# Three transformer blocks on one core: two unused tiles shift the moving operands in SBUF

## The chip, the cores and the metric

The kernel runs on one core of a Trainium2 chip. The metric is the device time in microseconds of one launch. The program is one straight sequence per engine: TensorE (PE, with its weight loads as PEld), VectorE (DVE), ScalarE (ACT), GpSimd (POOL) and SyncE (SP, which only issues DMAs). [...]

## The reference

Three blocks work in turn on x, 256 tokens of width 1024, in float32. Cut to what matters:

```
def swiglu(h, w_gate, w_up, w_down):            # d_ff = 2816
    return (silu(h @ w_gate) * (h @ w_up)) @ w_down

# blocks 0 and 1 (i = 0, 1)
x = x + 0.5 * swiglu(rms_norm(x, g[0]), ...)
h = rms_norm(x, g[1])
m = even_mixer(h, ...) if i == 0 else mla_mixer(h, ...)
x = x + m
x = x + 0.5 * swiglu(rms_norm(x, g[2]), ...)
x = x + rms_norm(sigmoid(rms_norm(x, g[3]) @ ple_w_gate) * (p_i @ ple_w_proj), g[4])

# block 2
mixed = concat(block attention, state-space mixer, pooling mixer) of rms_norm(x) @ w_in
x = x + mixed @ w_out
x = x + swiglu(rms_norm(x), ...)
out = rms_norm(x)
```

`even_mixer` has a gated spatial part and a chunked recurrence, `mla_mixer` is an attention with low-rank projections of queries and keys. Most of the arithmetic is the five feed-forward networks (FFNs): 1024 x 5632 for gate and up, 2816 x 1024 for down.

## The kernel before

The activations are kept transposed: x is eight tiles of 128 rows (features) by 256 columns (tokens). The weights, 220 pieces of 128 x 2048 floats in the order of their use, are streamed by SP into three buffers `wraw`. Each half piece is split in two by line 256 (ACT: the rounded part `whi`) and line 257 (DVE: the remainder `wlo`), into six buffers each of 128 x 1024.

Every product of the large projections is three matmuls of type fp32r: high part times high part, low activation times high weight, high activation times low weight. With `mm(out, l, r)` (line 163), l is the stationary operand, loaded by a LDWEIGHTS, and r the moving one. In the rows a matmul stands as `acc<-hh,whi`: the moving tile first, then the stationary tile. Three kinds of projection use it:
- `fm` (gate, up, down and most of the others): stationary is a 128 x 128 slice of `whi` or `wlo`, moving is a 128 x 256 slice of activations, so the result is again transposed. For gate and up the moving tiles are `hh0` to `hh7` (high parts of the normalized rows) and `hl0` to `hl7` (low parts). For down they are slices of `big` tiles, of which each holds the parts of two chunks of the gated product. An FFN has 44 chunks x 8 x 3 = 1056 matmuls in gate and up, and 8 x 22 x 3 = 528 in down.
- `out_proj` (the mixers' output projections): the same, with slices of `big` or, after attention, of `o2` as moving tile (the profile shows it as `o`).
- `tm` (projections whose result stands by tokens): stationary is a 128 x 128 slice of the activations, moving up to 512 columns of `whi` or `wlo`.

The order is as the loops write it, but for a few pieces that `high_priority` and `issue_after` move. In an FFN, gate and up run with two pauses early in the stretch: the sum of squares of x over the features is made on PE with a column of ones (`Stat.begin`), and the resulting scale is spread over the partitions by transposes of `ny` against `ident` (`Stat.finish`, line 299). After that, gate and up, and down behind them, go on without other work on PE; DVE and ACT evaluate what leaves PSUM and split the weights ahead.

Tiles get their place in SBUF by pool, `wp` first, then `cp`, then `sp`, and in a pool in the order in which a name is first asked for; a place is rounded up to 32 bytes per partition. In the built program the bytes per partition are:

```
tiles                                   start modulo 256, before    after
wraw, whi, wlo (wp)                                  128             128
cols (672 bytes, cp)                                 128             128
ones (4 bytes, cp)                                    32              32
x, ident, hh0..hh7, hl0..hl7 (cp)                     64             192
constants behind them, e.g. k_tri                    160              32
gu (sp, first)                                         0             128
sq, sqa, rb, sg, pr, big, o2, as (sp)                  0              64
ae, at (sp)                                          128             192
```

The slices that the matmuls take are multiples of 512 bytes into these tiles (but for a few behind a piece of 390 columns), so the table gives the operands' own places. `constants` (line 168) is where the tiles of the change are asked for; `run` and `build` follow it.

Of the kernel before, what the change touches and what calls it, by code (L numbers as in the profile page):

```python
# [10 lines left out]
FT = mybir.dt.float32  # L11
# [6 lines left out]
P = 128  # L18
# [88 lines left out]
class Kern:  # L107
# [61 lines left out]
    def constants(self):  # L169
        nc, a, cp = self.nc, self.a, self.cp  # L170
        self.cols = cp.tile([P, a["cols"].shape[1]], FT, name="cols")
        self.x = []
        self.raw = [self.wp.tile([P, PIECE], FT, name="wraw", bufs=3) for _ in range(2)]

        def load_x(c, n, eng=nc.sync):
            t = cp.tile([P, n * T], FT, name=f"x{c}")
            eng.dma_start(t, a["xT"][:, c * T : (c + n) * T])
            self.x += [t[:, u * T : (u + 1) * T] for u in range(n)]

        def load_w(i, q, n):  # L180
            o = slice(q * 512, (q + n) * 512)
            nc.sync.dma_start(self.raw[i][:, o], a["wts"][i][:, o])


        self.ones = cp.tile([P, 1], FT, name="ones")
        nc.vector.memset(self.ones, 1.0)
        idle = self.tmp(512, "gu", bufs=3)
        nc.vector.memset(idle, 0.0)
        ps = self.aux()
        for _ in range(5):  # L190
            self.mm(ps[:, :T], idle[:, :P], idle[:, :T])
        load_x(0, 1)
        nc.scalar.dma_start(self.cols, a["cols"])
        load_w(0, 0, 1)
        load_x(1, 1, nc.scalar)
        load_w(0, 1, 1)
        load_x(2, 1, nc.scalar)
        load_w(0, 2, 1)
        load_x(3, 1)
        load_w(0, 3, 1)  # L200
        load_x(4, 2)
        load_w(1, 0, 2)
        load_x(6, 2)
        load_w(1, 2, 2)
        self.ident = cp.tile([P, P], FT, name="ident")
        nc.sync.dma_start(self.ident, a["ident"])
        self.hT = [
            (cp.tile([P, T], FR, name=f"hh{c}"), cp.tile([P, T], FR, name=f"hl{c}"))
            for c in range(D)
        ]  # L210
        self.eps = cp.tile([P, 1], FT, name="eps")
        nc.vector.memset(self.eps, EPS)
        nc.scalar.activation(self.tiny(1, "nz"), self.ones, AF.Silu)
# [1435 lines left out]
```

## Time and profile before

| | before |
|---|---|
| runs | 1342.49, 1348.98, 1348.85 us |
| median | 1348.85 us |
| profiled execution | 1348.33 us |
| its span (first to last instruction) | 1346.5 us |
| PE busy | 1319.8 us, 98% of the span |
| weight loads (PEld) | 1290.1 us, 96% |
| DVE, ACT | 920.6 and 727.1 us |
| matmuls | 10830 |

A matmul's duration in the trace reaches from its start to the modelled end of its result. Successive matmuls overlap, so busy time and mean duration do not tell how fast they follow each other. The number of them in a window does. A float32 matmul that is not fp32r stands as two instructions.

### The profile page before, as it was taken

To read this page: it belongs to the slowest core of one execution; us is meant where nothing else is said; L and a number is where in the kernel's file an instruction comes from. 1 tells how busy PE (TensorE), PEld (TensorE's weight loads), DVE (VectorE), ACT (ScalarE), POOL (GpSimd) and SP (SyncE) were. 2 spreads that over 40 slices of the span, in tenths; PEclk is the share of its full clock that TensorE was granted. 3 is DMA by queue.
4 is the path that set the end of the run, shared out by engine and by line. 5 is a ranking of instruction groups with operands and counts; after the bars stand their busy time and mean duration, and the time that the engine had idled before them with its cause. 6 is when DMAs were issued, how large, how long until landed. Compare 5 with 4: busy or idle time off the path is not lost.

```text
span 1346.5 us, 25894 instructions
## 1 busy us (share of the span) xinstructions
PE 1319.8 (98%) x10830; PEld 1290.1 (96%) x10830; DVE 920.6 (68%) x1528; ACT 727.1 (54%) x1110; POOL 76.7 (6%) x94
## 2 busy tenths in 40 slices
PE   8999999999999999999999899999998999999997
PEld 8999999899999999999999679999998998999997
DVE  6866567968667557866656767766558897866643
ACT  6655446546544456655445666544445675644442
POOL 4000010002000001000010002000002000200001
PEclk9999999999999999999999999999999999999998
DMA  8755455345555453655455324555545343555541
GB/s 313 261 192 205 175 191 186 103 159 182 188 187 198 171 205 126 220 188 188 160 187 193 118 72 148 189 188 188 183 163 188 126 167 119 185 188 188 188 159 61
DMA packets 34933, 235.50 MB, mean 175 GB/s; under 512 B 4016, under 2 KB 4784, under 8 KB 7168
## 3 DMA queue, kind: packets, MB, share of 16 engines
q1 hardware_dynamic: 32976, 229.98, 49.1%
q0 software_dynamic: 832, 2.47, 0.6%
q8 instruction: 85, 1.39, 0.4%
q10 hardware_dynamic: 1008, 1.40, 0.3%
q14 instruction: 32, 0.26, 0.1%
HBM read 232.78 MB, written 1.05 MB: 174 GB/s over the span
## 4 chain that ended last, share of the span: by engine, by line
PE 74%; DVE 5%; ACT 2%; issue 1%; DVEq 0%; ACTq 0%
PE acc L163 70%; PE aux L163 4%; DVE wlo L257 2%; PE aux L299 0%; DVE big L1172 0%; PE aux L1127 0%; ACT whi L256 0%; DVE qs L958 0%; DVE kv L958 0%; DVE big L511 0%; ACT ae L1119 0%; ACT big L946 0%; ACT at L1129 0%; DVE big L1494 0%; DVE nz L293 0%
## 5 line engine op out<-in xcount | busy, mean ns | idle before, releaser
L257 DVE TENSOR_TENSOR wlo<-wraw,whi 128x1024 fp32r<-128x1024 f32 (+1 forms) x440 | 530.3, 1219 | 270.1 <-ACT whi L256 177.0
L256 ACT ACTIVATE whi<-wraw 128x1024 fp32r<-128x1024 f32 (+1 forms) x440 | 451.7, 1048 | 319.3 <-PE acc L163 224.9
L163 PE MATMUL acc<-hh,whi 128*128 128x256 f32 x2192 | 330.7, 281 | 4.1 <-ACT hh L535 3.1
L163 PE MATMUL acc<-hl,whi 128*128 128x256 f32 x2192 | 329.6, 280 | 0.2 <-DVE hl L540 0.2
L163 PE MATMUL acc<-hh,wlo 128*128 128x256 f32 x2192 | 328.8, 280 | 0.2 <-DVE wlo L257 0.2
L163 PEld LDWEIGHTS acc<-hh,whi 128*128 128x128 f32 x2192 | 288.5, 189 | 5.8 <-ACT hh L535 3.8
L163 PEld LDWEIGHTS acc<-hh,wlo 128*128 128x128 f32 x2192 | 288.7, 189 | 0.8 <-DVE wlo L257 0.6
L163 PEld LDWEIGHTS acc<-hl,whi 128*128 128x128 f32 x2192 | 288.6, 189 | 0.4 <-DVE hl L540 0.4
L163 PE MATMUL acc<-big,whi 128*128 128x256 f32 x2032 | 277.9, 283 | 0.0
L163 PEld LDWEIGHTS acc<-big,whi 128*128 128x128 f32 x2032 | 261.6, 189 | 0.4 <-ACT big L267 0.2
L163 PE MATMUL acc<-big,wlo 128*128 128x256 f32 x1016 | 164.8, 283 | 0.0
L163 PEld LDWEIGHTS acc<-big,wlo 128*128 128x128 f32 x1016 | 139.8, 189 | 0.0
L315 POOL TENSOR_TENSOR sqa<-sqa,sq 128x256 f32<-128x256 f32 x72 | 65.5, 910 | 1135.8 <-ACT sq L314 1133.7
L426 DVE TENSOR_TENSOR gu<-acc,rb 128x512 f32<-128x512 f32 (+1 forms) x122 | 81.9, 678 | 51.9 <-PE acc L163 51.9
L270 ACT ACTIVATE hh<-x,cols 128x256 fp32r<-128x256 f32 x64 | 30.3, 503 | 84.2 <-DVE x L465 80.6
L267 ACT ACTIVATE big<-pr 128x256 fp32r<-128x256 f32 x114 | 45.9, 409 | 51.9 <-DVE pr L444 50.1
L442 ACT ACTIVATE sg<-gu 128x256 f32<-128x256 f32 x110 | 44.8, 411 | 38.7 <-DVE gu L426 38.5
L268 DVE TENSOR_TENSOR big<-pr,big 128x256 fp32r<-128x256 f32 x114 | 47.9, 426 | 20.3 <-ACT big L267 20.2
L444 DVE TENSOR_TENSOR pr<-sg,gu 128x256 f32<-128x256 f32 x110 | 45.4, 418 | 2.8 <-ACT sg L442 2.8
L271 DVE SCALAR_TENSOR_TENSOR hl<-x,cols,hh 128x256 fp32r<-128x256 f32 x64 | 36.9, 602 | 8.5 <-ACT hh L270 8.3
L163 PE MATMUL aux<-big 128*128 128x128 f32 (+5 forms) x260 | 37.6, 310 | 1.9 <-DVE big L680 1.7
L314 ACT ACTIVATE sq<-x 128x256 f32<-128x256 f32 x62 | 24.0, 405 | 24.9 <-DVE x L467 18.4
(297 smaller groups left out, 788.1 us busy)
## 6 DMA issues: line engine op xcount, KB each, us to landing
wraw<-wts SPq DMA_DIRECT2D x216, 1024.0 KB, 4.9
wraw<-wts SPq DMA_DIRECT2D x4, 256.0 KB, 5.0
wraw<-wts SPq DMA_DIRECT2D x2, 512.0 KB, 6.5
x<-xT SPq DMA_DIRECT2D x2, 256.0 KB, 5.7
big<-wsT POOLq DMA_DIRECT2D x1, 512.0 KB, 10.4
gu<-pT ACTq DMA_DIRECT2D x2, 256.0 KB, 3.1
out<-big SPq DMA_DIRECT2D x2, 256.0 KB, 2.2
out<-big ACTq DMA_DIRECT2D x2, 256.0 KB, 2.4
```

The lines of the kernel that those rows point to most:

```text
L163: return self.nc.tensor.matmul(out, l, r, start=start, stop=stop, skip_group_check=True).ins
L256: nc.scalar.activation(hi[:, i], s, AF.Copy)
L257: nc.vector.tensor_tensor(lo[:, i], s, hi[:, i].bitcast(FT), op=OP.subtract)
L267: a = nc.scalar.activation(hi, src, AF.Copy)
L268: b = nc.vector.tensor_tensor(lo, src, hi.bitcast(FT), op=OP.subtract)
L270: a = nc.scalar.activation(hi, src, AF.Copy, scale=scale)
L271: b = nc.vector.scalar_tensor_tensor(lo, src, scale, hi.bitcast(FT), op0=OP.mult, op1=OP.subtract)
L314: nc.scalar.activation(q, src, AF.Square)
L315: self.mark = nc.gpsimd.tensor_tensor(self.sq[0], self.sq[0], q, op=OP.add).ins
L426: self.nc.vector.tensor_tensor(out.rearrange("p (u t) -> p u t", u=n), ps.rearrange("p (u t) -> p u t", u=n), rb.unsqueeze(1).to_broadcast ...
L442: self.mark = nc.scalar.activation(sg, gu[:, :T], AF.Silu).ins
L444: nc.vector.tensor_tensor(pr, sg, gu[:, T:], op=OP.mult)
```

## The change

Two tiles are asked for and never used: one of 32 floats (128 bytes per partition) in `cp` behind `ones`, and one of 48 floats (192 bytes) in `sp` behind `gu`. Everything that is asked for later in these pools moves up: the tiles in `cp` behind the first by 128 bytes, `gu` too, and the tiles in `sp` behind the second by 320. The weights stay. All engines have the same instructions in the same order; only the addresses differ, as the table above shows.

```
         self.ones = cp.tile([P, 1], FT, name="ones")
+        cp.tile([P, 32], FT, name="pad")
         nc.vector.memset(self.ones, 1.0)
         idle = self.tmp(512, "gu", bufs=3)
...
             (cp.tile([P, T], FR, name=f"hh{c}"), cp.tile([P, T], FR, name=f"hl{c}"))
             for c in range(D)
         ]
+
+        self.sp.tile([P, 48], FT, name="pad", bufs=1)
         self.eps = cp.tile([P, 1], FT, name="eps")
```

## Rows read from the trace of the kernel before

**Rows 1.** The page's first part: busy us of each engine.
```profile
PE 1319.8 (98%) x10830; PEld 1290.1 (96%) x10830; DVE 920.6 (68%) x1528; ACT 727.1 (54%) x1110; POOL 76.7 (6%) x94
```

**Rows 2.** The chain of waits, two long pieces: start us, us, what.
```profile
321.89 181.99 PE acc L163 x1536
...
550.14 174.82 PE acc L163 x1476
```

**Rows 3.** The page's second part, 40 slices: clock in tenths, GB/s.
```profile
PEclk9999999999999999999999999999999999999998
...
GB/s 313 261 192 205 175 191 186 103 159 182 188 187 198 171 205 126 220 188 188 160 187 193 118 72 148 189 188 188 183 163 188 126 167 119 185 188 188 188 159 61
```

**Rows 4.** The page's groups: line engine op tiles xcount | busy, mean ns | idle.
```profile
L257 DVE TENSOR_TENSOR wlo<-wraw,whi 128x1024 fp32r<-128x1024 f32 (+1 forms) x440 | 530.3, 1219 | 270.1 <-ACT whi L256 177.0
...
L163 PE MATMUL acc<-hh,whi 128*128 128x256 f32 x2192 | 330.7, 281 | 4.1 <-ACT hh L535 3.1
...
L163 PE MATMUL acc<-big,whi 128*128 128x256 f32 x2032 | 277.9, 283 | 0.0
...
L163 PE MATMUL acc<-big,wlo 128*128 128x256 f32 x1016 | 164.8, 283 | 0.0
```

**Rows 5.** Windows: gate/up, down of each FFN: window, length, busy (count), PEclk, ...
```profile
30.00:128.00 98.00, 98.00 (x867) 98.00 (x867) 71.96 (x99) 55.44 (x81) 1.10 (x1) 1.00 0.65 221
131.00:191.00 60.00, 60.00 (x508) 60.00 (x507) 32.27 (x43) 29.82 (x41) 4.42 (x6) 1.00 0.51 179
330.00:428.00 98.00, 98.00 (x835) 98.00 (x834) 64.91 (x88) 49.01 (x69) 0.58 (x1) 1.00 0.56 188
430.00:496.00 66.00, 66.00 (x553) 66.00 (x552) 39.03 (x53) 31.24 (x44) 5.16 (x7) 1.00 0.51 178
560.00:655.00 95.00, 95.00 (x809) 95.00 (x808) 64.76 (x87) 47.73 (x68) 0.00 (x0) 1.00 0.57 193
657.00:717.00 60.00, 60.00 (x502) 60.00 (x502) 30.97 (x36) 27.60 (x38) 4.43 (x6) 1.00 0.50 176
850.00:946.00 96.00, 96.00 (x817) 96.00 (x817) 64.62 (x86) 46.52 (x68) 0.00 (x0) 1.00 0.55 189
949.00:1009.00 60.00, 60.00 (x503) 60.00 (x501) 30.82 (x37) 27.81 (x38) 4.49 (x6) 1.00 0.50 176
1170.00:1271.00 101.00, 101.00 (x860) 101.00 (x859) 68.86 (x90) 49.30 (x72) 0.00 (x0) 1.00 0.54 183
1274.00:1333.00 59.00, 59.00 (x494) 59.00 (x493) 25.18 (x29) 26.58 (x35) 5.51 (x6) 1.00 0.36 126
```

**Rows 6.** Windows, PE alone: two hh stretches (first, third), two output projections.
```profile
215.50:236.90 21.40, 21.40 (x191) 1.00 0.57 197
292.80:303.70 10.90, 10.90 (x94) 1.00 0.45 153
...
531.50:543.00 11.50, 11.50 (x104) 1.00 0.01 3
...
1134.00:1147.90 13.90, 13.90 (x120) 1.00 0.44 152
```

**Rows 7.** The timeline behind a down projection, one by one: start us, us, ...
```profile
498.50 0.28 PE L163 MATMUL acc<-hh,wlo 128*128 128x256 f32 x1
...
501.22 0.28 PE L163 MATMUL acc<-hh,wlo 128*128 128x256 f32 x1
```

**Rows 8.** Matmuls with o2: durations ns min/median/max, first and last start us.
```profile
L163 PE MATMUL acc<-o,whi x176: 274/282/386, 785.2 to 1139.2; 128*128 128x256 f32 x176
...
L163 PE MATMUL acc<-o,wlo x88: 278/283/386, 786.8 to 1139.3; 128*128 128x256 f32 x88
```

**Rows 9.** The timeline where the weights move: start us, us, what xcount.
```profile
1107.24 1.07 PE L163 MATMUL acc<-whi,hl 128*128 128x256 f32 x8
1108.15 1.07 PE L163 MATMUL acc<-wlo,hh 128*128 128x256 f32 x8
...
1113.59 1.10 PE L163 MATMUL acc<-wlo,hh 128*128 128x256 f32 x8
```

More of the change, by code (lines that the diff above doesn't have):

```diff
@@ L185, in constants @@
         self.ones = cp.tile([P, 1], FT, name="ones")
+        cp.tile([P, 32], FT, name="pad")
         nc.vector.memset(self.ones, 1.0)
@@ L210, in constants @@
         ]
+        self.sp.tile([P, 48], FT, name="pad", bufs=1)
         self.eps = cp.tile([P, 1], FT, name="eps")
```

## Prediction

> **What bounds the kernel now.** I read the page's busy shares first: PE 1319.8 us of a span of 1346.5, DVE 920.6, ACT 727.1 [rows 1]. The chain of waits says the same: its longest pieces are nothing but matmuls of line 163, 182 us in a row without a step on another engine [rows 2]. [...] So neither clock nor DMA nor the splitting of the weights (530 us of DVE in all, 1219 ns for each half piece [rows 4]) sets the pace; what counts is the time from one matmul's start to the next.
>
> That step is not on the page, because the durations (281 ns and more) overlap. It comes out of windows cut inside steady stretches. The count x takes in matmuls that merely reach into the window; at a duration of about 280 ns and a step of about 118 ns those are 2.4. So the step is the window's length over (x - 2.4) [rows 5]:
> - gate and up projections (moving: hh or hl): 98/864.6 = 113.35 ns in the first FFN, then 117.7, 117.8, 117.8, 117.8 ns in the other four;
> - down projections (moving: big): 60/505.6 = 118.7 ns in the first, then 119.9, 120.1, 119.9, 120.0 ns.
>
> All of these are 128x256 with a 128x128 weight load beside each. [...] The output projections, with big or o2 as moving tile, take 10.9/91.6 = 119.0 and 13.9/117.6 = 118.2 ns. Shorter hh stretches outside the FFNs, 21.4/188.6 = 113.5 and 11.5/101.6 = 113.2 ns [rows 6]. An error of one in the count is 0.5 to 1% in these.
>
> Set beside the addresses: the weights stand at 128 modulo 256, hh and hl at 64 (192 ahead of the weights, or 64 behind), big and o2 at 0 (128 from them). Distance 64 has two levels, 113.4 and 117.8; distance 128 has two others, 118.7 and 120.0. The four FFNs at 117.8 run the same loops at the same addresses as the one at 113.4, so a level is not given by address alone. In the rows it holds to the end of a stretch, and it passes into the down projection: the only 113.4 is followed by the only 118.7. The opposite step is not a copy: the hh stretch that begins straight after a down projection of 120 ns runs from 498.50 to 501.22, 24 steps (the alternation hh, hl, hh is unbroken between the two rows shown), at 113.3 ns [rows 7].
>
> **The change part by part.** No instruction is added, removed or reordered on any engine; two tiles that nothing uses take 128 and 192 bytes. Weights stay. The rows x, ident, hh and hl go from 64 to 192 modulo 256, so that hh is now 64 ahead of the weights instead of 64 behind. Tiles after the second pad go from 0 to 64: big, o2 and the statistics are now 64 behind.
>
> *The tiles at 128 that go to 64.* These are 2032 + 1016 matmuls with big and 176 + 88 with o2 [rows 4, 8], 3312 together. Of them 5 x 22 x 8 x 3 = 2640 are the five down projections (528 each) and 672 the output and embedding projections. Big's new distance, 64 behind, is the one that hh has now, so I price it with hh's two levels.
> - Four down projections come straight after gate and up at 117.8; I take it that the level is carried, as it is now: 4 x 528 x (120.0 - 117.8) = -4.7 us. If they fell to 113.4 it would be -13.9.
> - The first comes after 113.4: 528 x (118.7 - 113.4) = -2.8 us; -0.5 if it ran at 117.8.
> - The 672 others open after attention or vector work, where the hh stretches of [rows 6] are at 113.5: 672 x (118.7 - 113.4) = -3.6 us; -0.6 at 117.8.
>
> *hh and hl from 64 behind to 64 ahead.* The 2192 matmuls of the row shown [rows 4] and as many in each of the other two products, 6576 in all, have no direct row at this distance. The nearest is a projection with the roles changed: there the weights move and hh is stationary, so the moving tile is 64 ahead. Eight matmuls of 1.07 us are (1.07 - 0.28)/7 = 113 ns, and after a pause eight of 1.10 us are 117 ns [rows 9]: both levels of now, no third one. So I take the levels as unchanged and the term as 0. Its bounds: the first FFN's gate and up lose the low level, 1056 x 4.4 = +4.7 us; the four others gain it, 4 x 1056 x 4.4 = -18.6 us.
>
> *What is lost behind a down projection.* If down now runs at 117.8 and hands that on, three openings of 48 matmuls that are at 113.3 now (the 24 steps of [rows 7] lie in one) lose 4.4 ns each: 3 x 48 x 4.4 = +0.6 us. Below, 0.
>
> Matmuls with other shapes, ACT, DVE and DMA have the same instructions; no row ties their times to an address, and none is on the long pieces of the chain: 0, and a us either way as bound. A PE 1% faster asks 1% more of the weight stream, 190 instead of 188 GB/s, which the start exceeds.
>
> Sum: -4.7 - 2.8 - 3.6 + 0.6 = -10.5 us on a span of 1346.5, so 1336 us, or 1348.33 - 10.5 = 1337.8 as the profiled execution's own time. That execution is 0.5 us under the median of 1348.85, so the time after is 1338 us. The three runs of before are 1342.49, 1348.98 and 1348.85: the gap of 6.4 us is about one FFN on the other level (1056 x 4.4 + 528 x 1.3 = 5.3 us), which fits a level that differs from execution to execution.
>
> **The rivals.**
> *More stretches lock to the low level (1310 to 1331 us).* With all tiles at 64, an FFN's gate, up and down share a level, so one more FFN at 113.4 is worth 1584 x 4.4 = 7.0 us beyond the 1338; all four are 28, so 1310. For it: 64 ahead has shown 113, and the level seems set when PE starts again after the two statistics pauses, whose own operands move too. Against it: four of five long stretches are at 117.8 now, with hh already at distance 64.
>
> *The address is not the cause: 1349 us.* Big and hh differ in more than their place (loop, tile width, who writes them). If 120 belongs to the down projection itself, nothing moves. Against it: three families at 128, of different code, are all at 118 to 120, and hh in various code is at 113.4 or 117.8 only. [...]
>
> *64 ahead is not as good as 64 behind (1358 us).* Here the direction matters: hh, 64 ahead of the weights, meets the load as big does now and runs at 119.9. Its five long stretches average (113.35 + 4 x 117.8)/5 = 116.9 ns, so 6576 x 3.0 = +20 us, against -10.5 for big: +9.5. It decides once the new step of hh is over 118.5 ns. For it: the first hh term has only a row with changed roles. Against it: that row shows 113 and 117.
>
> **How the numbers follow.** The forecast (levels stay, big joins them, an FFN more or less on the low level: 1331 to 1345) has 0.45; more low stretches 0.25; no effect of the address 0.20; the wrong direction 0.10. Half a per cent, 6.7 us, is about what a measurement tells from no change. Faster by more: 0.38 of the forecast's 0.45 and all of the second, 0.63. Within it: 0.07 of the forecast, 0.18 of the third and 0.02 of the fourth, 0.27. Slower: 0.02 of the third, since levels vary, and 0.08 of the fourth, 0.10. The range goes from 1310, every FFN low, to 1352, no effect with the first FFN on the high level; the forecast's own is 1331 to 1345.
>
> **What would show it.** Down projections at 113.4 or 117.8 ns in windows of 60 us (x near 531 or 512, now about 503) prove the main term; 120 there refutes it. Gate and up at 113.4 or 117.8 prove the 0 term; a third level refutes it. An FFN whose two parts are on different levels shows that the level is not carried. The count of FFNs on the low level decides between 1338 and 1310, and I would be most wrong there.

## The result and the profile after

The changed kernel takes 1332.8 us (median of six runs, 1330.09 to 1336.2) against 1348.91 for the kernel before (1342.49 to 1353.84): a ratio of 0.9888, 95% interval 0.9863 to 0.9913. The forecast was 1338. The profiled execution took 1331.74 us, with a span of 1330.0 against 1346.5, so 16.5 us have to be found.

The page's busy shares and its groups for the changed kernel answer to [rows 1, 4]. The columns are those of before.

```profile
PE 1305.2 (98%) x10830; PEld 1275.3 (96%) x10830; DVE 922.9 (69%) x1528; ACT 726.4 (55%) x1110; POOL 76.1 (6%) x94
...
L163 PE MATMUL acc<-big,whi 128*128 128x256 f32 x2032 | 271.7, 280 | 0.0
```

DVE and ACT are busy as long as before, within 0.3%. The gain is on PE, and the windows inside the FFNs show where. Here they are for the changed kernel, gate/up and down in turn as in [rows 5] (window, PE busy with its count, then the other engines, granted clock, DMA share, GB/s):

```profile
30.00:128.00 98.00, 98.00 (x835) 98.00 (x834) 70.12 (x97) 52.90 (x78) 1.09 (x1) 1.00 0.64 218
135.00:193.00 58.00, 58.00 (x495) 58.00 (x494) 31.08 (x41) 28.25 (x40) 4.41 (x6) 1.00 0.52 182
330.00:428.00 98.00, 98.00 (x835) 98.00 (x834) 65.46 (x91) 50.28 (x72) 0.58 (x1) 1.00 0.55 186
434.00:496.00 62.00, 62.00 (x549) 62.00 (x549) 38.20 (x53) 31.26 (x44) 5.13 (x7) 1.00 0.54 188
555.00:650.00 95.00, 95.00 (x841) 95.00 (x840) 68.54 (x95) 51.92 (x75) 0.00 (x0) 1.00 0.61 202
653.00:712.00 59.00, 59.00 (x503) 59.00 (x502) 30.43 (x37) 27.87 (x37) 4.41 (x6) 1.00 0.50 179
840.00:936.00 96.00, 96.00 (x849) 96.00 (x849) 68.20 (x89) 48.49 (x71) 0.00 (x0) 1.00 0.57 189
940.00:999.00 59.00, 59.00 (x504) 59.00 (x503) 30.96 (x37) 27.95 (x38) 4.48 (x6) 1.00 0.52 179
1160.00:1256.00 96.00, 96.00 (x849) 96.00 (x849) 68.20 (x89) 48.15 (x71) 0.00 (x0) 1.00 0.56 190
1260.00:1318.00 58.00, 58.00 (x495) 58.00 (x494) 24.43 (x27) 25.65 (x35) 5.49 (x6) 1.00 0.37 128
```

PE is busy for the whole of each window, at a granted clock of 1.00, with a DMA share of 0.37 to 0.64. Window over (count - 2.4) gives the step, from one matmul's start to the next. Gate/up: 117.7, 117.7, 113.3, 113.4, 113.4 ns, where it was 113.35 once and 117.7 to 117.8 four times. Down: 117.7, 113.4, 117.9, 117.6, 117.7 ns, where it was 118.7 to 120.1. There are the two levels of 113.4 and 117.8 and no third, and in these windows the steps of 119 and more are gone. With 528 matmuls in a down projection and some 910 in the long part of a gate/up, this is down -0.5 - 3.4 - 3 x 1.2 = -7.5 us and gate/up +4.0 - 3 x 4.0 = -8.0 us.

The shorter stretches answer to [rows 6]; in the same order, for the changed kernel:

```profile
219.00:240.00 21.00, 21.00 (x181) 1.00 0.57 201
296.00:306.50 10.50, 10.50 (x92) 1.00 0.46 145
531.00:542.00 11.00, 11.00 (x96) 1.00 0.01 1
1123.00:1136.00 13.00, 13.00 (x117) 1.00 0.48 160
```

The two hh stretches went from 113 up to 21/178.6 = 117.6 and 11/93.6 = 117.5 ns, the output projections down to 10.5/89.6 = 117.2 and 13/114.6 = 113.4. By these windows the others about cancel. Down and gate/up are 15.5 of the 16.5 us; the last microsecond I have not placed.

From here the two steps are called the low level (113.4) and the high level (117.8).

### The profile page after: what moved, and what is told of

Same layout as the page of the kernel before. It is cut to its first block, busy times and chain, and to the rows that moved or that the text cites. A ratio compares the mean times of both kernels' runs of the same rounds, so it can differ in the third digit from the quotient of the medians.

```text
span 1330.0 us, 25894 instructions
## 1 busy us (share of the span) xinstructions
PE 1305.2 (98%) x10830; PEld 1275.3 (96%) x10830; DVE 922.9 (69%) x1528; ACT 726.4 (55%) x1110; POOL 76.1 (6%) x94
## 4 chain that ended last, share of the span: by engine, by line
PE 74%; DVE 5%; ACT 2%; issue 1%; DVEq 0%; ACTq 0%
PE acc L163 69%; PE aux L163 4%; DVE wlo L260 1%; PE aux L302 0%; ACT whi L259 0%; PE aux L1130 0%; DVE big L1175 0%; DVE qs L961 0%; ACT hh L273 0%; ACT at L1132 0%; DVE kv L961 0%; ACT ae L1122 0%; ACT big L949 0%; DVE big L514 0%; DVE big L429 0%
## 5 line engine op out<-in xcount | busy, mean ns | idle before, releaser
L163 PE MATMUL acc<-big,whi 128*128 128x256 f32 x2032 | 271.7, 280 | 0.0
L163 PEld LDWEIGHTS acc<-big,whi 128*128 128x128 f32 x2032 | 256.4, 189 | 0.4 <-ACT big L270 0.2
L163 PE MATMUL acc<-big,wlo 128*128 128x256 f32 x1016 | 161.7, 280 | 0.0
```

Source lines behind the costliest of these rows:

```text
L163: return self.nc.tensor.matmul(out, l, r, start=start, stop=stop, skip_group_check=True).ins
```

## The experiments

Four questions: does the down projection take the level of gate/up; which of the two pads does what; which distances have these levels; what sets the level? Theory 1, which no run shows directly, is that the level is set when a stretch starts, kept while nothing changes, and moved when the distance changes. That it is a phase against the weight load, as the expectations have it, is my assumption; the runs show only the steps.

**Both 64 ahead (a_both_ahead).** The changed kernel with a smaller second pad, so that big stands where hh does.

```
-        self.sp.tile([P, 48], FT, name="pad", bufs=1)
+        self.sp.tile([P, 16], FT, name="pad", bufs=1)
```

> Second pad 16 floats instead of 48: hh, hl and now big, o2 too stand 64 bytes ahead of the weights. Theory 1 (a stretch has the level 113.4 or 117.8 ns, and it flips where the sign of the distance changes between gate/up and down): without the change of sign, down keeps the level of its gate/up, so the three FFNs whose gate/up ran at 113.3 in the changed kernel have down at 113.4 too; 3 x 528 x 4.4 = 7 us less than the changed kernel's 1332.8, less 2.5 us for the one FFN that had flipped to its favour: about 1328. Rival 2 (down projections have a level of their own by their loop, 117.8): down at 117.8 after gate/up at 113.3, time about 1333. Rival 3 (level is drawn at each start of a stretch): mixed, 1326 to 1337.

Measured: 1331.25 us, the median of six from 1321.03 to 1345.05; the ratio, without the slowest, is 0.9859 (0.9808 to 0.9909). The profiled execution is that slowest one. Two FFNs in it, gate/up and down, PE alone (window, busy and count, clock, DMA share, GB/s):

```profile
555.00:657.00 102.00, 102.00 (x869) 1.00 0.60 203
661.00:719.00 58.00, 58.00 (x495) 1.00 0.53 182
1172.00:1271.00 99.00, 99.00 (x875) 1.00 0.57 192
1275.00:1331.00 56.00, 56.00 (x497) 1.00 0.38 133
```

117.7 is followed by 117.7, 113.5 by 113.2; the other three FFNs are high in both parts. So down has no level of its own, and rival 2 falls. As the two parts now share one draw, an FFN is worth about 6.4 us (some 910 and 528 matmuls at 4.4 ns), and the six runs are as far apart as three or four FFNs. The median is not the 1328 that I expected: it depends on how many FFNs are low.

**Both 64 behind (b_both_behind).** hh as in the kernel before, big moved by 64 only; the edit is against the kernel before.

```
+        self.sp.tile([P, 16], FT, name="pad", bufs=1)
```

> No first pad, second pad 16 floats: hh stays 64 behind the weights as before, big and o2 go from 128 to 64 behind. This is the priced term of the prediction by itself, with the level carried. Theory 1: gate/up as before (mostly 117.8, perhaps one FFN at 113.4), down on the same level as its gate/up, none at 119 to 120: 1349 - 4.7 - 2.8 - 3.6 + 0.6 = about 1338. Rival 2 (down's own level 117.8): about the same, 1339 to 1341, with down at 117.8 even behind 113.4. Rival 3: mixed. A rival that the first pad brings all: 1349, down at 120.

Measured: 1339.6 us, 1328.48 to 1347.03, ratio 0.9938 (0.991 to 0.9965). Third and fourth FFN:

```profile
552.00:654.00 102.00, 102.00 (x869) 1.00 0.60 203
658.00:716.00 58.00, 58.00 (x495) 1.00 0.52 182
842.00:940.00 98.00, 98.00 (x867) 1.00 0.57 194
944.00:1001.00 57.00, 57.00 (x506) 1.00 0.54 186
```

117.7 and 117.7, then 113.4 and 113.2: again the level is carried, and one FFN of five is low, as before. This is the priced term of the prediction by itself, and it came out at 1339.6 against 1338.

**The second pad alone (c_second_pad_alone).** The changed kernel without the first: hh 64 behind, big 64 ahead.

```
-        cp.tile([P, 32], FT, name="pad")
```

> The second pad of the change by itself: hh stays 64 behind, big and o2 stand 64 ahead (moved by 192). Theory 1: gate/up as before (mostly 117.8), and the change of sign flips the level, so that down behind 117.8 runs at 113.4: 4 x 528 x 6.6 = 13.9 us less and about 0.5 for the first FFN, others 2 to 3: about 1332 to 1334. Rival 2 (own level of down): down at 117.8, about 1339 to 1341. Rival 3: mixed.

Measured: 1340.51 us, 1337.32 to 1344.39, ratio 0.9944 (0.9924 to 0.9965). Second and third FFN:

```profile
325.00:421.00 96.00, 96.00 (x849) 1.00 0.57 190
425.00:488.00 63.00, 63.00 (x538) 1.00 0.51 178
544.00:646.00 102.00, 102.00 (x869) 1.00 0.59 204
650.00:708.00 58.00, 58.00 (x495) 1.00 0.52 182
```

The hh stretches that open straight behind these two downs, first and last matmul of each (start us, us, what):

```profile
490.81 0.28 PE L163 MATMUL acc<-hh,whi 128*128 128x256 f32 x1
496.15 0.28 PE L163 MATMUL acc<-hh,wlo 128*128 128x256 f32 x1
...
710.63 0.28 PE L163 MATMUL acc<-hh,whi 128*128 128x256 f32 x1
716.16 0.28 PE L163 MATMUL acc<-hh,wlo 128*128 128x256 f32 x1
```

Low is followed by high (113.4, then 117.6), but high by high too (117.7, 117.7). My "flip" is wrong: from gate/up to down across a change of sign the low level does not survive, and the high level mostly stays. Over this kernel and the changed one, all five low gate/ups were followed by a high down, and of five high ones four stayed high and one became low (the second FFN of the changed kernel). Yet the step of a down does not tell all: behind the two downs that followed a low gate/up the next hh stretch is low again, (496.15 - 490.81)/47 = 113.6 ns, and behind the two that followed a high one it is high, (716.16 - 710.63)/47 = 117.7. All four downs run at 117.6 to 117.8, so in c something of the first state outlasts them; in the changed kernel all four such openings are high. That the spread of c is small because down is high whatever was drawn fits, but was not tested.

**The first pad alone (d_first_pad_alone).** The changed kernel without the second: hh 64 ahead, big level with the weights (distance 0).

```
-        self.sp.tile([P, 48], FT, name="pad", bufs=1)
```

> The first pad of the change by itself: hh 64 ahead of the weights, big and o2 at 128 modulo 256, the weights' own place (distance 0, which no run has shown). Theory 1 with a period of 128 bytes: distance 0 is like distance 128, down at 118.7 to 120.0; gate/up at 113.3 in about three FFNs (two more than before, 2 x 1056 x 4.4 = 9.3 us): about 1340. If distance 0 is a place of its own (period 256), down has a third step, possibly over 120: over 1345 at 125 ns. Rival: ahead is no better than behind for hh; gate/up mostly 117.8, 1349.

Measured: 1350.09 us, 1341.56 to 1357.28, ratio 1.0011 (0.9985 to 1.0036): no change. Third FFN, and the hh stretch that opens straight behind the second FFN's down:

```profile
556.00:653.00 97.00, 97.00 (x858) 1.00 0.62 210
658.00:717.00 59.00, 59.00 (x494) 1.00 0.52 179
...
500.40:505.40 5.00, 5.00 (x45) 1.00 0.44 143
```

Gate/up at 113.4, down at 59/491.6 = 120.0: distance 0 costs what 128 costs, also behind a low gate/up. The opening is at 5/42.6 = 117.4 ns. At the same place [rows 7] had 113.3. So the step from 0 to 64 ahead ends high, the step from 128 to 64 behind ends low (four of four openings behind a down, in d's trace and in that of before). The profiled execution took 1341.56 us, the least of twelve, and has four low gate/ups; by their times the others had fewer: at 4.0 us for each, an execution at the median of 1350.09 has about two (an estimate).

**Two more distances (e_behind96, f_behind32).**

```
-        cp.tile([P, 32], FT, name="pad")
-        self.sp.tile([P, 48], FT, name="pad", bufs=1)
+        cp.tile([P, 56], FT, name="pad")     # e: 96 behind; f: 8 instead of 56: 32 behind
+        self.sp.tile([P, 16], FT, name="pad", bufs=1)
```

> Pads of 56 and 16 floats: hh, hl, big and o2 all stand 96 bytes behind the weights (at 32 modulo 256; the weights at 128). If the two levels belong to every distance but 0 and 128: gate/up and down at 113.3 or 117.8, carried into down, 1322 to 1346. If a distance has its own levels: a third step. The few matmuls that stand 88 behind in the kernel before ran at 113 among neighbours at 113; if that distance has the low level alone, all at 113.3 and about 1310. Theory 'only 64 is good': 119 to 120, 1349 or more.

> Pads of 8 and 16 floats: hh, hl, big and o2 all stand 32 bytes behind the weights (at 96 modulo 256). If the two levels belong to every distance but 0 and 128: 113.3 or 117.8, 1322 to 1346. If 32 is near enough to 0 to meet the weight load as 0 does: 120 throughout, 1349 + 6576 x 3 ns = about 1365. In the changed kernel the few matmuls that stand 40 ahead of the weights run at 120 among neighbours at 117.8, which speaks for the latter.

Measured: 1355.63 us for e (ratio 1.0061, 1.0042 to 1.008; eleven of twelve executions from 1352.93 to 1358.63, the other, at 2616.68, left out of the ratio and unexplained) and 1354.23 us for f (1.0041, 1.0025 to 1.0058). First and second gate/up of e:

```profile
27.00:131.00 104.00, 104.00 (x889) 1.00 0.64 218
...
327.00:430.00 103.00, 103.00 (x871) 1.00 0.55 185
```

and the first gate/up and down of f:

```profile
27.00:131.00 104.00, 104.00 (x881) 1.00 0.64 216
134.00:194.00 60.00, 60.00 (x510) 1.00 0.51 180
```

At 96 behind there are two steps, 117.3 and 118.6, at 32 behind a single one, 118.4 and 118.2, with runs within 2.7 us. For e the second of the expectations fits, that a distance has its own levels; for f neither of the two does. Both distances have steps of their own, and no low level. The few matmuls at 88 behind that ran at 113 may only have been carried by their neighbours. Of the distances run, 64 alone has the low level.

In every run the weights stand at 128, so these runs by themselves do not tell a distance from a place of the moving tile. What speaks for the distance is few matmuls: in [rows 9] the moving tile is the weights' own, at 128, beside hh at 64, and the step is 113 or 117 ns; big at 128 beside the weights at 128 has 120.0 (d). Weights at another place were not run.

**Twelve matmuls at distance 128 behind the pause (g_twelve_far).** As b; `lev` is a tile of 64 columns at 0 modulo 256, filled once at the start (not shown) and read four times over. The extra products are not used.

```
                     stat.finish(m)
+                    if len(chunks) == 44:
+                        far = self.aux()[:, :T].rearrange("p (r c) -> p r c", r=4)
+                        with self.behind(m):
+                            for _ in range(12):
+                                self.mm(far, l, self.lev.unsqueeze(1).to_broadcast([P, 4, 64]))
```

> As b_both_behind, but behind the second pause of each FFN twelve extra matmuls (result unused) whose moving tile stands at distance 128, then gate/up go on at 64 behind. Theory 1 (the level is set by where the weight load stands when a stretch starts, and the step from distance 128 to 64 behind leads to the low level: all six such transitions without a pause in the kernel before went to 113): gate/up at 113.3 in all five FFNs and, at the same sign, down too; five times 12 x 120 ns = 7 us of extra work, 1339.6 + 7 - about four FFNs x 7 us = 1318 to 1320, with less spread from run to run. Rival (the level is drawn at random whatever ran before): levels as in b, 1339.6 + 7 = 1347.

Measured: 1325.81 us, 1321.05 to 1332.38, ratio 0.9838 (0.98 to 0.9876). Three of its five gate/ups and a down:

```profile
31.00:130.00 99.00, 99.00 (x876) 1.00 0.62 213
324.00:424.00 100.00, 100.00 (x885) 1.00 0.58 193
428.00:489.00 61.00, 61.00 (x540) 1.00 0.54 187
546.00:644.00 98.00, 98.00 (x868) 1.00 0.61 205
```

113.3, 113.3, 113.2 ns and 113.5 in down; the fourth and fifth FFN are the same. In b one gate/up of five was low, in this execution five of five are. It took 1323.33 us; others took up to 1332.38, so not every execution need have all five low, and the smaller spread that I expected is not there. The timeline of the third restart (start us, us, what, count):

```profile
542.50 0.38 PE L303 MATMUL aux<-ident,ny 128*128 128x128 f32 x2
542.64 1.66 PE L163 MATMUL aux<-lev,whi 128*128 128x256 f32 x12
544.13 0.63 PE L163 MATMUL acc<-hl,whi 128*128 128x256 f32 x4
544.60 1.07 PE L163 MATMUL acc<-hh,wlo 128*128 128x256 f32 x8
```

The pause, twelve far ones, four at 64 behind in which the step settles ((0.63 - 0.28)/3 = 117 ns), then (1.07 - 0.28)/7 = 113. The extra work is 60 matmuls, 7 us; the median lies 6 to 8 us over the 1318 to 1320 that I expected.

**Two of them (i_two_far).**

```
-                            for _ in range(12):
+                            for _ in range(2):
```

> As g_twelve_far, with two extra matmuls behind the second pause instead of twelve (result unused). Theory 1 (a push of the phase is enough, as the single far matmul in 24 of h_one_far does it): gate/up and down at 113.3 in all five FFNs as with twelve, with 5 x 10 x 120 ns = 6 us less of extra work: about 1320. Rival (the stretch must first settle on the steps of distance 128, which takes about ten matmuls): some FFNs at 117.8, 1325 to 1339, with a spread of 7 us and more.

Measured: 1321.92 us, 1315.71 to 1329.36, ratio 0.9807 (0.9771 to 0.9843). First, second and third gate/up:

```profile
28.00:131.00 103.00, 103.00 (x877) 1.00 0.64 217
326.00:426.00 100.00, 100.00 (x884) 1.00 0.57 193
549.00:650.00 101.00, 101.00 (x860) 1.00 0.59 202
```

117.8, 113.4, 117.8, and the last two are low (113.3 each): two are not always enough. The time is lower than with twelve, but levels differ again between FFNs of one execution.

**One tile of sixteen at distance 128 (h_one_far).** As b, without extra work; 1 matmul in 24 of gate/up stands far.

```
-            for c in range(D)
+            for c in range(D - 1)
         ]
+        last = cp.tile([P, T], FR, name="hh7")
+        cp.tile([P, 48], FT, name="pad")
+        self.hT.append((last, cp.tile([P, T], FR, name="hl7")))
+        cp.tile([P, 16], FT, name="pad2")
```

> As b_both_behind, but the last of the sixteen tiles, hl7, stands at distance 128, so that one matmul in 24 of gate/up meets the weights from there. Theory 1: each one pushes the stretch toward the low level, 113 to 114.5 ns on the mean in all gate/up stretches, down at the level in which gate/up end (113.3): 1315 to 1325. Rival (one matmul is too short to move the level, it costs its own 120 and the stretch falls back): levels as in b, 1340. Second rival: it pushes each low stretch up, all at 117.8, 1345.

Measured: 1316.08 us, 1315.26 to 1317.17, ratio 0.9763 (0.9736 to 0.979). First gate/up and down, second gate/up, last down:

```profile
28.00:128.00 100.00, 100.00 (x878) 1.00 0.66 224
132.00:188.00 56.00, 56.00 (x496) 1.00 0.54 189
321.00:421.00 100.00, 100.00 (x878) 1.00 0.57 191
...
1247.00:1302.00 55.00, 55.00 (x488) 1.00 0.38 133
```

114.2 ns in every gate/up, which is the low level and 0.8 ns for the far one and the few steps behind it, and 113.5 and 113.3 in down. No FFN of this profile is high, and the six runs lie within 2 us. This is the fastest kernel here, 16.7 us under the changed one.

**The opposite push (j_one_level_with).** As a (64 ahead), with hl7 at distance 0; it is asked for ahead of `cols`, at 128 modulo 256.

```
+        first = cp.tile([P, T], FR, name="hl7")
         self.cols = cp.tile([P, a["cols"].shape[1]], FT, name="cols")
...
-            for c in range(D)
+            for c in range(D - 1)
         ]
+        self.hT.append((cp.tile([P, T], FR, name="hh7"), first))
```

> As a_both_ahead (all 64 ahead of the weights), but the last of the sixteen tiles, hl7, stands at 128 modulo 256, level with the weights (distance 0), so that one matmul in 24 of gate/up meets the weights from there. Theory 1 (the direction of the step counts): the step from distance 0 to 64 ahead led to 117.8 in all eight transitions without a pause in d_first_pad_alone, so every pass pushes to the high level: gate/up and down at 117.8 in all five FFNs, about 1345 to 1347, with little spread. Rival (any odd matmul shakes a stretch into the low level, as in h_one_far): 114 and 113.3, about 1316.

Measured: 1348.98 us, ratio 1.0002 (0.9984 to 1.0019); eleven of twelve executions from 1348.38 to 1351.13, the other, at 3693.27, left out of the ratio and unexplained. First gate/up and down, second gate/up:

```profile
30.00:130.00 100.00, 100.00 (x850) 1.00 0.62 214
134.00:194.00 60.00, 60.00 (x512) 1.00 0.50 179
332.00:430.00 98.00, 98.00 (x833) 1.00 0.55 185
```

118.0, 117.7 and 118.0, and 117.8 to 118.0 in the other three gate/ups: every FFN is high, where a, without the push, had one low in its profile and, by its times, up to four in other runs. The time is 2 us over what I expected. So an odd matmul as such does not help; as theory 1 has it, the direction of the step counts. In h and j the distance of the odd tile and the side of the others both differ, and a tile at 128 among others 64 ahead was not run.

**The changed kernel again (k_again).** No edit.

> The changed kernel again, for one more profile. Theory 1 (the level is set at each restart by a phase that differs between executions): other FFNs than in the first profile on the low level, or another count, with each FFN's level 4.65 us in gate/up; 1330 to 1336. Rival (the level is fixed by the program): gate/up low in the third, fourth and fifth FFN again.

Measured: 1330.45 us, one run. First, second and third gate/up in this execution:

```profile
30.00:128.00 98.00, 98.00 (x868) 1.00 0.65 222
330.00:428.00 98.00, 98.00 (x834) 1.00 0.57 191
555.00:649.00 94.00, 94.00 (x831) 1.00 0.60 204
```

The first is at 113.2 here, and at 117.7 in the other profile of the same program; the second is high (117.8 here) and the third low (113.4) in both, the fourth and fifth low as well (113.3). A level is not fixed by the program.

## Why the prediction was right, point by point

**Big at 64 has hh's two levels.** Right: no stretch of the changed kernel is left at 119 to 120 in the windows, and experiment b has this step alone, at 1339.6 us (ratio 0.9938, 0.991 to 0.9965).

**The level is carried into the down projection.** This step failed for the changed kernel. I took carrying for a property of the stretch; it was seen where the distance keeps its sign (ten of ten FFNs in a and b, two of them low, and the second FFN of g, low in both parts). The change puts hh ahead and big behind, and there no low level survived. The first term (four downs at 117.8, -4.7 us) came out at -3.4 - 3 x 1.2 = -7.0 us, because one down went low; the other three went to 117.8 as priced, but behind a low gate/up instead of a high one. The second (-2.8 us) came out at -0.5. The total, -7.5 us in both cases, is a coincidence.

**hh from behind to ahead: 0, between +4.7 and -18.6.** Mis-sized. It measured -8.0 us in the profiled execution: three low gate/ups instead of one. The two levels were right, the odds not. Over the profiles, gate/up 64 ahead was low in 12 of 20 FFNs (changed kernel twice, a, d), 64 behind in 4 of 15 (before, b, c). That the side changes the odds is not shown by these counts: four of the twelve come from the fastest of d's executions, and by their times d has about two low ones at its median where the changed kernel has three and four in its two profiles, with hh in the same place. What sets the odds stays open; the operands of the statistics pauses move too. By itself the first pad gained nothing measurable at the median (d): its profile is 6.8 us under that of before, but most of its executions have fewer low gate/ups, and the hh matmuls outside the long stretches took about 5 us more than before, by their starts in the two traces.

**The 672 others at 113.4 (-3.6 us).** Half right: the last output projection is at 113.4, the even mixer's at 117.2. Not foreseen was that the shorter hh stretches would go from 113 to 117.6, which took back as much.

**Openings behind down (+0.6 us).** Right in kind: the openings are at 117.8 in the changed kernel, four instead of the three that were priced.

**The rivals.** "More low stretches" is half of what happened: two more gate/ups, but their downs did not follow. "The address is not the cause" is refuted: b, e, f and h have the instructions of the kernel before in the same order and differ in places alone, and lie between 1316 and 1356 us. The same shape, at a granted clock of 1.00, has steps from 113.2 to 120.1 ns, and they change with the place of its operands; what on the chip makes them change, no row shows. "Ahead is worse" is refuted by d, with 64 ahead at 113.4.

The forecast of 1338 lies 5.2 us above the measured 1332.8. That it is so near is in part luck: down came out at its -7.5 us although the carrying behind it failed, gate/up gave 8.0 us where the sum had nothing, and all the others gave about 1 us where 3.0 were priced.

## What to carry to other kernels

Where PE is busy throughout (98% of the span here) and yet the steps of one shape differ (113.4 to 120.1 ns in the kernel before), count matmuls in windows, stretch by stretch, and set the steps beside the operands' places in SBUF before looking for a wait. A spread between runs can come from a state that is set at a restart and then kept (here about 4.0 us for a gate/up, 6.4 with its down): take two profiles of one program and compare them stretch by stretch. Such a state could be steered here: with all moving operands 64 behind the weights, one odd tile at distance 128 held the faster level (h, 114.2 ns with the odd one counted in); with all 64 ahead, one at distance 0 held the slower one (j, 117.7 to 118.0 ns). Whether this carries over to another kernel was not run.

## What the runs showed of the hardware

- The step of a 128x256 fp32r matmul with a 128x128 weight load, at a granted clock of 1.00, by the moving tile's distance from the weights in bytes, with the weights at 128 throughout (distances are written modulo 256; no run shows that 256 is the period): 0: 120.0 ns; 64 on either side: 113.4 or 117.8; 128: 118.7 or 120.0; 96 behind: 117.3 or 118.6; 32 behind: 118.4.
- At 64 both levels last for hundreds of matmuls (some 910 in a gate/up); they were seen to change only where PE pauses or the distance changes. Two executions of one program can differ in them (first gate/up of the changed kernel: 117.7 and 113.2).
- Changes without a pause: from 128 to 64 behind led to the low level in 5 of 5 gate/up stretches of g's profile (113.2 to 113.3 ns), behind twelve matmuls, and in 3 of 5 of i's (113.3 to 113.4), behind two; from 0 to 64 ahead to the high one (d 117.4, j 117.7 to 118.0). From 64 behind to 64 ahead and back (c), a low level came back, 113.4, 117.6, 113.6. What makes the two levels was not measured, nor were the steps at 32 and 96 ahead.
